# Hybrid decoder step: sample states of the gated-delta layer as the moving operand, 32-column strips stationary, results used in place

## The chip, the cores and the metric

The kernel runs on one NeuronCore of a Trainium2 chip. The metric is the device time of one execution in microseconds (us); lower is better. Before the change the median of three runs is 2275.27 us (2274.68 to 2281.68).

## What is computed

One inference step of a four-layer decoder trunk (retention, Mamba-2 SSD, gated DeltaNet, retention), each layer followed by a squared-ReLU MLP. 256 prompt tokens and 8 sample sequences of 4 tokens each go through the same weights, so that every dense product has 288 token columns. Only the gated-delta layer (the third) is touched, and in it only the sample part. For one sample sequence and one of the 16 heads, with the state S (128 x 128) from the input, the reference does this over its single chunk of four tokens:

```python
v_new = u_c - jnp.einsum('bhtk,bhkv->bhtv', w_c, S)
o_c = jnp.einsum('bthk,bhkv->bthv', qd_c, S) + jnp.einsum('bhts,bhsv->bthv', attn_c, v_new)
S = S * cd_c[..., None, None] + jnp.einsum('bshk,bhsv->bhkv', kd_c, v_new)
```

`u_c` and `w_c` are the solutions of a unit lower triangular 4 x 4 system per head and sequence (right sides: values and decayed keys, both times beta). `o_c` is then normalised over its 128 elements. Two heads that follow each other share q and k.

## The kernel before

Everything is fp32. The large dense products (`dense`, lines 190 to 227) take their weights through `raw` tiles from HBM, split each into a rounded part `wh` (ACT, L207) and a rest `wl` (DVE, L210), and do three matmuls per 128 x 128 weight tile with 288 moving columns (L222, L223, L224, output `psd`). These fill most of the program; the scans of the mixers are put between them.

The gated-delta layer works in four units of four heads (`units`). A unit m has `proj(m)` (dense products and convolution for q, k, v), `prep(m)` (grams, the triangular inverses, gates), `loop(m)` (the prompt scan in two chunks), `sample(m)` (the sample sequences), `gate(m)` and `fin(m)`, and the output product `out`. `weave` runs prep and loop as a chain; each of their yields is a wait that is filled with dense blocks, `proj(m+1)` and `sample(m)` (both in turn), in the fourth unit with `sample(3)` alone after `gate(3)` and `out(1)`. The yields of `sample` count as filled time. A scheduler then sets the final order of each engine's instructions, so that the order on an engine is not that of the code; two PSUM banks carry the tag `s`, which `sample` and the small matmuls of `prep` use in turn.

`sample(m)` (lines 1570 to 1612) goes over two pairs of heads. For each head it loads the eight states as `St` (128 x 8 x 128, L1584) and does eight matmuls with a state as the stationary operand and eight columns of `qk` (k and q, four tokens each) as the moving one:

```python
for b in range(DB):
    mm(pv[:, h, b], St[:, b], qk[:, pr:4:2, SEQ + b:T:DB])
yield 1.8
```

The result `ps_kS` is (value index x columns). ACT copies it into `kS` in two pieces (L1590), two matmuls with the identity transpose it (`ps_u2`), DVE forms the right side `r2` with a scale and the values `vb2` (L1595), ACT scales the q part to `qo` (L1597), one matmul with the inverse `Y2` gives v_new (`ps_n2`, copied to `x4`, L1601), one with `at2` gives the inner part (`ps_o2`), and DVE adds `qo` to make `o2` (L1605). Square and sum (L1608), the mean (DVE, L1610), a power on POOL (L263) and a scaled copy to `on2` (L1612) finish it; `fin` transposes `on2` (L1730) for the gate. All matmuls of this layer's scan go through the helper `mm` at L1296. In the trace buffer names lose trailing digits: `ps_u2` is ps_u, `ps_n2` ps_n, `ps_o2` ps_o (with input lkv, which is `x4`), `Y2` Y, `at2` at, `o2` o, `on2` on.

`prep` makes `sc2`, `vb2`, `Y2` (the inverse, transposed) and `at2`; `er` is a small tile of decays (L1387) that POOL multiplies with q into `qd`.

Of the kernel before, what the change touches and what calls it, by code (L numbers as in the profile page):

```python
# [8 lines left out]
F32 = mybir.dt.float32  # L9
F32R = mybir.dt.float32r  # L10
I32 = mybir.dt.int32
AF = mybir.ActivationFunctionType
ALU = mybir.AluOpType
# [3 lines left out]
SEQ = 256  # L17
DB, DS = 8, 4
NS = DB * DS
T = SEQ + NS  # L20
# [15 lines left out]
def make_consts():  # L36

    f = np.float32
    c = {}
# [3 lines left out]
    u = np.arange(NS)  # L43
# [5 lines left out]
    t = np.arange(SEQ)  # L49
# [39 lines left out]
    x = np.arange(128)  # L89
# [18 lines left out]
    c["gdn_lms"] = np.stack(lms, axis=1).astype(f)  # L108
    same = jx[:, None] == ub[None, :]
    c["gdn_m4"] = np.stack([same & (jt[:, None] <= ut[None, :]), same & (ut[None, :] < jt[:, None])], axis=1).astype(f)  # L110
    u1 = np.zeros((128, 2, 128), f)
    for h in range(4):
        for blk in range(4):
# [10 lines left out]
class K:  # L124
# [1119 lines left out]
    def gdn(self, ctx, j, i):  # L1244
# [5 lines left out]
        V, A, G, PE = nc.vector, nc.scalar, nc.gpsimd, nc.tensor  # L1250
        ident = self.ident

        def cload(name):
            a = I[name]
            t = cp.tile(list(a.shape), F32, name="c_" + name)
            nc.sync.dma_start(t, a)
            return t

        b32, lms, gmask, m4, xi0, h16 = (cload(n) for n in ("gdn_b32", "gdn_lms", "gdn_gm", "gdn_m4", "gdn_x0", "gdn_h16"))
        i4, s4 = m4[:, 0], m4[:, 1]  # L1260
        istk = cp.tile([128, 16], F32, name="istk")
        nc.sync.dma_start(istk, I["ssd_istk"][:, 0:16])
# [29 lines left out]
        def bcm(ap, n):  # L1292
            return ap.unsqueeze(1).broadcast_to([ap.shape[0], n, ap.shape[1]])

        def mm(o, l, r, start=True, stop=True):
            PE.matmul(o, lhsT=l, rhs=r, start=start, stop=stop)  # L1296
# [57 lines left out]
        T64 = rp.tile([64, 8, 64], F32, name="T64")  # L1354
        G.memset(T64, 0.0)

        def proj(m):
            qk = rp.tile([128, 4, T], F32, name="qk", tag="qk", bufs=2)
            v = [rp.tile([128, T], F32, name="v", tag=f"v{a}") for a in range(4)]
            tails, tl = [], rp.tile([128, 8, 35], F32, name="tl", tag="tl", bufs=2)  # L1360
            for (c0, dst) in ((m * 256, [qk[:, 0], qk[:, 1]]), (1024 + m * 256, [qk[:, 2], qk[:, 3]]), (2048 + m * 512, v)):
                yield from self.conv_dense(rp, xh, xl, w[:, c0:c0 + len(dst) * 128], c0 // 128, rb, cw, cb, None, dst, tails, tl)
            units[m] = {"qk": qk, "v": v, "tails": tails}
# [7 lines left out]
        def prep(m):  # L1371
# [4 lines left out]
            for kh in range(2):  # L1376
                ps = self.ps("ps_dif", "s")
                h0 = 4 * m + 2 * kh
                for r in range(2):
                    mm(ps[:, r * 256:(r + 1) * 256], e2[:, h0 + r:h0 + r + 1].broadcast_to([128, 128]), cts)  # L1380
                Et = rp.tile([128, 2, 2, 128], F32, name="Et", tag=f"Et{kh}")
                pv = ps.rearrange("p (r t y) -> p r t y", r=2, t=2)
                for r in range(2):
                    for tt in range(2):
                        A.activation(Et[:, r, tt], pv[:, r, tt], AF.Abs, bias=nct[:, tt, h0 + r:h0 + r + 1])
                er = rp.tile([128, 2, 128], F32, name="er", tag="er")
                A.activation(er, pv[:, :, 1], AF.Exp)  # L1387
                e_ = Et.rearrange("p r t y -> p (r t y)")
                A.activation(e_, e_, AF.Exp, scale=-1.0)
                G.tensor_tensor(out=qd[:, 2 * kh:2 * kh + 2], in0=er, in1=bcm(qk[:, kh, 128:256], 2), op=ALU.mult)  # L1390
                Es.append(Et)
            rb2 = rp.tile([128, 32], F32, name="rb2", tag="rb2")
            V.tensor_scalar(out=rb2, in0=i4, scalar1=g2[:, m:m + 1], scalar2=None, op0=ALU.mult)
            ps = self.ps("ps_dif2", "s")
# [154 lines left out]
            def expand(k, t):  # L1549
# [16 lines left out]
            at2 = rp.tile([128, 128], F32, name="at2", tag="at2")  # L1566
            G.tensor_tensor(out=at2.rearrange("p (c y) -> p c y", c=4), in0=bcm(sm[:, 0], 4),
                            in1=b32.rearrange("p (c y) -> p c y", c=4), op=ALU.mult)
            u.update(Tm=Tm, L=L, at=Es, qd=qd, kd=kd, vb=vbs, ncf=ncf, eq=eq, sc2=sc2, Y2=Y2, x4=x4, vb2=vb2, at2=at2)

        def sample(m):
            u = units[m]
            while "x4" not in u:
                yield None
            qk, Y2, x4, vb2, at2, sc2, eq = (u[n] for n in ("qk", "Y2", "x4", "vb2", "at2", "sc2", "eq"))
            on2 = u["on2"] = rp.tile([128, 128], F32, name="on2", tag="on2")
            for pr in range(2):
                hp = slice(64 * pr, 64 * pr + 64)

                pT = self.ps("ps_kS", "s")  # L1580
                pv = pT[:, 0:128].rearrange("p (h b c) -> p h b c", h=2, b=DB)
                for h in range(2):
                    St = rp.tile([128, DB, 128], F32, name="St", tag="St", bufs=3)
                    nc.sync.dma_start(St, I["state_gdn"][j, :, 4 * m + 2 * pr + h].rearrange("b k v -> k b v"))  # L1584
                    for b in range(DB):
                        mm(pv[:, h, b], St[:, b], qk[:, pr:4:2, SEQ + b:T:DB])
                    yield 1.8
                kS = rp.tile([128, 2, 64], F32, name="kS", tag="kS", bufs=2)
                for a in range(2):
                    A.copy(kS[:, a].rearrange("p (h t b) -> p h b t", h=2, b=DB), pv[:, :, :, 4 * a:4 * a + 4])  # L1590
                pu = self.ps("ps_u2", "s")
                for a in range(2):
                    mm(pu[hp, a * 128:(a + 1) * 128], kS[:, a], ident)
                qo, r2, o2 = (rp.tile([128, 128], F32, name=n_, tag=n_) for n_ in ("qo", "r2", "o2"))
                V.scalar_tensor_tensor(out=r2[hp], in0=pu[hp, 128:256], scalar=sc2[hp, 2:3], in1=vb2[hp], op0=ALU.mult,  # L1595
                                       op1=ALU.add)
                A.activation(qo[hp], pu[hp, 0:128], AF.Copy, scale=eg2[hp, m:m + 1])  # L1597
                yield 1.0
                pn = self.ps("ps_n2", "s")
                mm(pn[hp, 0:128], Y2[hp, hp], r2[hp])  # L1600
                A.copy(x4[hp, 1], pn[hp, 0:128])  # L1601
                yield 1.0
                po = self.ps("ps_o2", "s")
                mm(po[hp, 0:128], at2[hp, hp], x4[hp, 1])
                V.tensor_tensor(out=o2[hp], in0=qo[hp], in1=po[hp, 0:128], op=ALU.add)  # L1605
                yield 1.0
                oo = rp.tile([128, 1], F32, name="oo1", tag="oo1", bufs=2)
                A.activation(qo[hp], o2[hp], AF.Square, accum_out=oo[hp])  # L1608
                ms = rp.tile([128, 1], F32, name="ms1", tag="ms1", bufs=2)
                V.scalar_tensor_tensor(out=ms[hp], in0=oo[hp], scalar=1.0 / 128, in1=eq[hp, 4:5], op0=ALU.mult, op1=ALU.add)  # L1610
                r = self.rsqrt(ms, hp)
                A.activation(on2[hp], o2[hp], AF.Copy, scale=r[hp])  # L1612

        def loop(m):
            u = units[m]
# [212 lines left out]
```

## Time and profile before

| | |
|---|---|
| median of three runs | 2275.27 us |
| the profiled execution | 2272.98 us, of which the span from first to last instruction is 2271.1 us |
| mean granted TensorE clock | 0.978 |
| gated-delta layer | about 1096 to 1497 us of the span |

The engines are PE (matmul) with PEld (its weight loads), DVE (VectorE), ACT (ScalarE), POOL (GpSimd) and SP (which issues most transfers). A row of the timeline gives the start, the length from the first start to the last end, and how many instructions were merged; lengths of neighbours overlap, because matmuls are pipelined, so that the pace is read from start to start. A group of matmuls carries its array shape (rows\*columns used by the stationary operand) and the moving operand. An fp32 matmul of the scan stands in the trace as two records; those of `psd` as one.

### The profile page before, as it was taken

To read this page: it belongs to the slowest core of one execution; us is meant where nothing else is said; L and a number is where in the kernel's file an instruction comes from. 1 tells how busy PE (TensorE), PEld (TensorE's weight loads), DVE (VectorE), ACT (ScalarE), POOL (GpSimd) and SP (SyncE) were. 2 spreads that over 40 slices of the span, in tenths; PEclk is the share of its full clock that TensorE was granted. 3 is DMA by queue.
4 is the path that set the end of the run, shared out by engine and by line. 5 is a ranking of instruction groups with operands and counts; after the bars stand their busy time and mean duration, and the time that the engine had idled before them with its cause. 6 is when DMAs were issued, how large, how long until landed. Compare 5 with 4: busy or idle time off the path is not lost. (4 is left out here: it accounts for less than half of the span.)

```text
span 2271.1 us, 43130 instructions
## 1 busy us (share of the span) xinstructions
PE 2186.3 (96%) x16332; PEld 2019.0 (89%) x16332; DVE 1562.4 (69%) x3211; ACT 1243.3 (55%) x2827; POOL 580.0 (26%) x605
## 2 busy tenths in 40 slices
PE   9999999998999999999898999989999999999998
PEld 7878899997889889999788987889999878889998
DVE  6777775557888877555886686466766677776554
ACT  4444455554767765545566566366644345445454
POOL 2100113332332222333322122034433001103333
PEclk9999999999999999999899999799999999999999
DMA  7876755545446545545443432257765666664553
GB/s 207 266 255 205 246 186 165 167 153 157 139 146 178 170 128 167 167 150 167 126 133 100 131 120 81 84 156 241 234 204 183 226 231 215 239 232 149 167 167 114
DMA packets 404076, 394.83 MB, mean 174 GB/s; under 512 B 12988, under 2 KB 353573, under 8 KB 403773
## 3 DMA queue, kind: packets, MB, share of 16 engines
q1 hardware_dynamic: 403708, 391.82, 54.3%
q8 instruction: 128, 2.10, 0.4%
q14 instruction: 80, 0.65, 0.1%
q10 hardware_dynamic: 96, 0.20, 0.0%
q0 software_dynamic: 64, 0.07, 0.0%
HBM read 333.36 MB, written 58.69 MB: 173 GB/s over the span
## 5 line engine op out<-in xcount | busy, mean ns | idle before, releaser
L207 ACT CAST wh<-raw 128x512 fp32r<-128x512 f32 x1024 | 627.8, 621 | 687.5 <-PE psd L223 642.5
L210 DVE TENSOR_TENSOR wl<-raw,wh 128x512 fp32r<-128x512 f32 x1024 | 744.3, 734 | 316.3 <-ACT wh L207 292.9
L222 PE MATMUL psd<-xh,wh 128*128 128x288 f32 x2576 | 775.4, 302 | 6.4 <-ACT xh L297 4.6
L224 PE MATMUL psd<-xh,wl 128*128 128x288 f32 x2576 | 771.6, 300 | 4.7 <-DVE wl L210 4.3
L223 PE MATMUL psd<-xl,wh 128*128 128x288 f32 x2576 | 771.0, 300 | 4.0 <-DVE xl L298 3.2
L222 PEld LDWEIGHTS psd<-xh,wh 128*128 128x128 f32 x2576 | 487.1, 189 | 25.1 <-issue 9.6
L223 PEld LDWEIGHTS psd<-xl,wh 128*128 128x128 f32 x2576 | 490.6, 190 | 17.6 <-issue 8.1
L224 PEld LDWEIGHTS psd<-xh,wl 128*128 128x128 f32 x2576 | 489.4, 190 | 13.4 <-DVE wl L210 7.6
L222 PE MATMUL psd<-ah,wh 128*128 128x288 f32 x1536 | 463.5, 302 | 10.0 <-DVE sg L543 3.7
L224 PE MATMUL psd<-ah,wl 128*128 128x288 f32 x1536 | 460.5, 300 | 4.1 <-DVE wl L210 4.0
L223 PE MATMUL psd<-al,wh 128*128 128x288 f32 x1536 | 461.6, 301 | 0.4 <-DVE al L465 0.4
L222 PEld LDWEIGHTS psd<-ah,wh 128*128 128x128 f32 x1536 | 293.9, 192 | 18.9 <-DVE x L442 4.2
L223 PEld LDWEIGHTS psd<-al,wh 128*128 128x128 f32 x1536 | 294.0, 191 | 9.6 <-issue 7.4
L224 PEld LDWEIGHTS psd<-ah,wl 128*128 128x128 f32 x1536 | 294.6, 192 | 7.6 <-DVE wl L210 5.5
L482 POOL TENSOR_TENSOR x<-x,dn 128x288 f32<-128x288 f32 x120 | 149.2, 1243 | 233.2 <-DVE dn L480 233.2
L463 POOL TENSOR_TENSOR a<-v 128x288 f32<-128x288 f32 x128 | 110.2, 861 | 271.9 <-ACT v L462 267.6
L726 DVE SCALAR_TENSOR_TENSOR S<-S,ps_up 128x512 f32<-128x512 f32 x128 | 83.5, 685 | 53.4 <-PE ps_up L725 50.7
L827 DVE SCALAR_TENSOR_TENSOR cacc<-U,cw,cacc 128x312 f32<-128x312 f32 x192 | 106.4, 561 | 8.2 <-ACT cacc L822 5.9
L465 DVE TENSOR_TENSOR al<-a,ah 128x288 fp32r<-128x288 f32 x128 | 59.0, 461 | 67.2 <-POOL a L463 66.5
L263 POOL TENSOR_TENSOR rs_y<-ms,mhalf 128x3 f32<-128x3 f32 (+3 forms) x37 | 36.7, 995 | 237.6 <-DVE ms L742 170.6
L803 POOL COPY U<-cb 128x24 f32<-128x24 f32 x64 | 34.1, 538 | 218.0 <-DVE cacc L827 120.5
L480 DVE TENSOR_TENSOR dn<-psd,rb 128x288 f32<-128x288 f32 x128 | 58.2, 455 | 40.0 <-PE psd L224 40.0
(504 smaller groups left out, 2651.7 us busy)
## 6 DMA issues: line engine op xcount, KB each, us to landing
raw<-mlp_w_up SPq DMA_DIRECT2D x64, 1024.0 KB
raw<-mlp_w_down SPq DMA_DIRECT2D x64, 1024.0 KB
raw<-ret_w_in SPq DMA_DIRECT2D x32, 1024.0 KB
S<-state_ret SPq DMA_DIRECT2D x64, 512.0 KB
s_ret<-S SPq DMA_DIRECT2D x64, 512.0 KB
raw<-ssd_w_in SPq DMA_DIRECT2D x24, 1024.0 KB
raw<-gdn_w_in SPq DMA_DIRECT2D x24, 1024.0 KB
raw<-ret_w_in SPq DMA_DIRECT2D x32, 512.0 KB
```

The source lines that it names most:

```text
L207: self.last_cast = nc.scalar.copy(wh, src)
L210: nc.vector.tensor_tensor(out=wl, in0=src, in1=wh, op=ALU.subtract)
L222: nc.tensor.matmul(po, lhsT=hs[k][:, os], rhs=xh[k], start=(k == 0), stop=False)
L223: nc.tensor.matmul(po, lhsT=hs[k][:, os], rhs=xl[k], start=False, stop=False)
L224: self.last_mm = nc.tensor.matmul(po, lhsT=ls[k][:, os], rhs=xh[k], start=False, stop=(k == kt - 1))
L263: self.nc.gpsimd.tensor_tensor(out=y[rows], in0=ms[rows], in1=self.mhalf[rows].broadcast_to([rows.stop - rows.start, n]), op=ALU.pow)
L463: nc.gpsimd.tensor_tensor(out=a, in0=v, in1=v, op=ALU.mult)
L465: nc.vector.tensor_tensor(out=al[o], in0=a, in1=ah[o], op=ALU.subtract)
L480: nc.vector.tensor_tensor(out=t, in0=ps, in1=rb2, op=ALU.mult)
L482: e.tensor_tensor(out=self.x[o], in0=self.x[o], in1=t, op=ALU.add)
L726: nc.vector.scalar_tensor_tensor(out=S[:, b, z], in0=S[:, b, z], scalar=C["g4"][h], in1=up, op0=ALU.mult, op1=ALU.add)
L827: nc.vector.scalar_tensor_tensor(out=acc[:, 0:n], in0=u, scalar=wk, in1=acc[:, 0:n], op0=ALU.mult, op1=ALU.add)
```

## The change

- In `sample` the state `St[:, b]` becomes the moving operand (128 columns). Stationary is a strip of 32 columns from a new tile `Z`, in which the k and q columns of sequence b stand at their places and all else is zero. Sequence b writes the partitions 32\*(b % 4) and up of `ps_kS`; b and b + 4, and the two heads, accumulate into the same strip. The result is (rows x value index), already the right way round.
- `ps_u2`, `r2`, `qo` (as a scaled q part) and `o2` go. The rows of `kS` are used in place: `prep` makes `WQ`, two 128 x 128 matrices that hold the scaled inverse and the scaled identity with their rows scattered by a constant `pm` (two matmuls `ps_wq`, two ACT scalings and an ACT copy per unit). `ps_n2` and `ps_o2` become two accumulating matmuls each: `WQ` by `kS` and the earlier one.
- The square and the final scaling read `ps_o2` in PSUM, which so stays taken until `on2` is written.
- POOL fills `Z` (four copies per unit and a memset at the layer's start); `er` is written into `qd` and multiplied there in place.
- The yield after a head's matmuls goes from 1.8 to 1.0; the one behind `kS` stays at 1.0. One constant of 128 KB more is loaded.

```diff
+        Z = rp.tile([128, 2, DB, 40], F32, name="Z")
+        G.memset(Z, 0.0)
...
-                er = rp.tile([128, 2, 128], F32, name="er", tag="er")
+                er = qd[:, 2 * kh:2 * kh + 2]
...
+            for pr in range(2):
+                for bh in range(2):
+                    bs = slice(4 * bh, 4 * bh + 4)
+                    G.tensor_copy(Z[:, pr, bs, 8:40].rearrange("p b (a x) -> p b a x", a=2)[:, :, :, bs],
+                                  qk[:, pr:4:2, SEQ:T].rearrange("p a (t b) -> p b a t", b=DB)[:, bs])
...
+            t0, t1 = self.t128("wy"), self.t128("wq")
+            A.activation(t0, Y2, AF.Copy, scale=sc2[:, 2:3])
+            A.activation(t1, ident, AF.Copy, scale=eg2[:, m:m + 1])
+            WQ = rp.tile([128, 2, 128], F32, name="WQ", tag="WQ")
+            ps = self.ps("ps_wq", "s")
+            for a, t in enumerate((t0, t1)):
+                mm(ps[:, 128 * a:128 * a + 128], pm[:, a], t)
+            A.copy(WQ.rearrange("p a x -> p (a x)"), ps[:, 0:256])
...
                     for b in range(DB):
-                        mm(pv[:, h, b], St[:, b], qk[:, pr:4:2, SEQ + b:T:DB])
-                    yield 1.8
-                kS = rp.tile([128, 2, 64], F32, name="kS", tag="kS", bufs=2)
-                for a in range(2):
-                    A.copy(kS[:, a].rearrange("p (h t b) -> p h b t", h=2, b=DB), pv[:, :, :, 4 * a:4 * a + 4])
-                pu = self.ps("ps_u2", "s")
-                for a in range(2):
-                    mm(pu[hp, a * 128:(a + 1) * 128], kS[:, a], ident)
-                qo, r2, o2 = (rp.tile([128, 128], F32, name=n_, tag=n_) for n_ in ("qo", "r2", "o2"))
-                V.scalar_tensor_tensor(out=r2[hp], in0=pu[hp, 128:256], scalar=sc2[hp, 2:3], in1=vb2[hp], op0=ALU.mult,
-                                       op1=ALU.add)
-                A.activation(qo[hp], pu[hp, 0:128], AF.Copy, scale=eg2[hp, m:m + 1])
+                        c = 32 * (b % 4)
+                        mm(pT[c:c + 32, 0:128], Z[:, pr, b, 8 - 8 * h:40 - 8 * h], St[:, b], h == 0 and b < 4, h == 1 and b > 3)
+                    yield 1.0
+                kS = rp.tile([128, 128], F32, name="kS", tag="kS", bufs=2)
+                A.copy(kS, pT[:, 0:128])
                 yield 1.0
                 pn = self.ps("ps_n2", "s")
-                mm(pn[hp, 0:128], Y2[hp, hp], r2[hp])
+                mm(pn[hp, 0:128], WQ[:, 0, hp], kS, True, False)
+                mm(pn[hp, 0:128], Y2[hp, hp], vb2[hp], False, True)
                 A.copy(x4[hp, 1], pn[hp, 0:128])
                 yield 1.0
                 po = self.ps("ps_o2", "s")
-                mm(po[hp, 0:128], at2[hp, hp], x4[hp, 1])
-                V.tensor_tensor(out=o2[hp], in0=qo[hp], in1=po[hp, 0:128], op=ALU.add)
+                mm(po[hp, 0:128], WQ[:, 1, hp], kS, True, False)
+                mm(po[hp, 0:128], at2[hp, hp], x4[hp, 1], False, True)
```

Two places of the order on PE. The names are those of the trace; psd are the dense products, ps_kS the matmuls with the states, ps_u the transposes with the identity, ps_n and ps_o as above, ps_W (first two forms) and ps_v small matmuls of `prep`.

The first place is in the fourth unit: the second pair of heads before the change.

```order
L1296 MATMUL ps_o_18703<-lkv,at_18439 64x128
L1296 MATMUL ps_kS<-qk,St 128x8 x16
L224 MATMUL psd<-ah_17880,wl 128x288
L222 MATMUL psd<-ah_17881,wh 128x288
L223 MATMUL psd<-al_17885,wh 128x288
L1296 MATMUL ps_u_18737<-c_ident,kS 64x128
L224 MATMUL psd<-ah_17881,wl 128x288
L222 MATMUL psd<-ah_17882,wh 128x288
L223 MATMUL psd<-al_17886,wh 128x288
L1296 MATMUL ps_u_18737<-c_ident,kS 64x128
```

And the same unit, from the end of the first pair's chain to the second pair's states, with the change:

```order
L1302 MATMUL ps_n_18697<-kS,WQ 64x128
L1302 MATMUL ps_n_18697<-vb_18378,Y_18405 64x128
L1302 MATMUL ps_o_18701<-kS,WQ 64x128
L227 MATMUL psd<-ah_17875,wh 128x288
L228 MATMUL psd<-al_17879,wh 128x288
L1302 MATMUL ps_o_18701<-lkv,at_18436 64x128
L1302 MATMUL ps_kS<-St,Z 32x128 x8
L229 MATMUL psd<-ah_17875,wl 128x288
L1302 MATMUL ps_W_18216<-Ls,L 32x16 x32
L1548 MATMUL ps_v<-c_ident,v 128x128 x4
L1302 MATMUL ps_W_18216<-Ls,Tm 32x16 x32
L1548 MATMUL ps_v<-c_ident,v 128x128 x4
```

The transposes are gone, the two heads of the pair no longer stand in one run of 16, and the small matmuls of `prep` come between them.

The second place is the end of the fourth unit, `fin(3)`: before the change

```order
L1728 MATMUL ps_oT<-c_ident,on 128x128 x2
L1729 MATMUL ps_oT<-c_ident,on 128x128 x2
L1728 MATMUL ps_oT<-c_ident,on 128x128
L1729 MATMUL ps_oT<-c_ident,on 128x128
L1730 MATMUL ps_oT<-c_ident,on_18631 128x32 x3
L1728 MATMUL ps_oT<-c_ident,on 128x128
L1729 MATMUL ps_oT<-c_ident,on 128x128
L1730 MATMUL ps_oT<-c_ident,on_18631 128x32
```

and with it, from the row that follows 16 dense rows behind the first `ps_oT`:

```order
L1748 MATMUL ps_oT<-c_ident,on 128x128
L227 MATMUL psd<-ah_17876,wh 128x288
L1748 MATMUL ps_oT<-c_ident,on 128x128
L228 MATMUL psd<-al_17880,wh 128x288
L229 MATMUL psd<-ah_17876,wl 128x288
L227 MATMUL psd<-ah_17877,wh 128x288
L1747 MATMUL ps_oT<-c_ident,on 128x128
L1748 MATMUL ps_oT<-c_ident,on 128x128
L228 MATMUL psd<-al_17881,wh 128x288
```

Before, no dense row stood among the transposes; now 16 stand behind the first two of them and 11 more among the rest.

## Rows read from the trace of the kernel before

**Rows 1.** The page: engine, busy us (share of the span), instructions.
```profile
PE 2186.3 (96%) x16332; PEld 2019.0 (89%) x16332; DVE 1562.4 (69%) x3211; ACT 1243.3 (55%) x2827; POOL 580.0 (26%) x605
```

**Rows 2.** A stretch: its us, PE, PEld, DVE, ACT, POOL busy; clock, DMA share, GB/s.
```profile
1180.00:1216.00 36.00, 35.07 (x443) 31.45 (x441) 22.40 (x57) 24.07 (x70) 6.29 (x11) 1.00 0.33 100
```

**Rows 3.** Who PE waited for, 1096 to 1482 us: total us, times, longest.
```profile
PE ps_Y L1554 <- DVE T L1553: 4.2, 2, 3.0
```

**Rows 4.** Timeline of PE around the first head's states: start us, length us.
```profile
1168.36 0.29 PE L224 MATMUL psd<-xh,wl 128*128 128x288 f32 x1
1168.49 1.84 PE L1296 MATMUL ps_kS<-qk,St 128*128 128x8 f32 x16
1170.19 0.38 PE L222 MATMUL psd<-xh,wh 128*128 128x288 f32 x1
1170.40 0.29 PE L223 MATMUL psd<-xl,wh 128*128 128x288 f32 x1
```

**Rows 5.** Timeline of PE around eight matmuls with 32 stationary, 128 moving columns.
```profile
1140.89 0.29 PE L224 MATMUL psd<-xh,wl 128*128 128x288 f32 x1
1141.11 0.65 PE L1296 MATMUL ps_qs<-c_ident,qk 128*32 128x128 f32 x16
1141.69 0.40 PE L222 MATMUL psd<-xh,wh 128*128 128x288 f32 x1
1141.92 0.29 PE L223 MATMUL psd<-xl,wh 128*128 128x288 f32 x1
```

**Rows 6.** Timeline of PE around strips whose moving operands differ (retention).
```profile
77.00 1.05 PE L717 MATMUL ps_yi<-S,qm 128*32 128x512 f32 x4
77.98 0.40 PE L223 MATMUL psd<-xl,wh 128*128 128x288 f32 x1
```

**Rows 7.** Timeline of PE around the two transposes ps_u.
```profile
1178.32 0.29 PE L224 MATMUL psd<-xh,wl 128*128 128x288 f32 x1
1178.54 0.65 PE L1296 MATMUL ps_u<-c_ident,kS 128*64 128x128 f32 x4
1179.12 0.40 PE L222 MATMUL psd<-xh,wh 128*128 128x288 f32 x1
```

**Rows 8.** Timeline of PE around one matmul ps_n.
```profile
1356.40 0.43 PE L1296 MATMUL ps_n<-r,Y 64*64 64x128 f32 x2
1356.76 0.40 PE L222 MATMUL psd<-xh,wh 128*128 128x288 f32 x1
```

**Rows 9.** Timeline of PE around four full matmuls with 128 moving columns.
```profile
1469.32 1.05 PE L1296 MATMUL ps_vn<-vb,Ye 128*128 128x128 f32 x8
1470.13 0.38 PE L224 MATMUL psd<-ah,wl 128*128 128x288 f32 x1
```

**Rows 10.** Groups of instructions, ACT: a 128x128 scaling; busy us, mean ns, idle before.
```profile
L1542 ACT ACTIVATE vb<-ps_v,sc 128x128 f32<-128x128 f32 x4 | 1.5, 363 | 1.2 <-PE ps_v L1296 1.2
```

**Rows 11.** The page's groups, POOL: a small copy (columns as in Rows 10).
```profile
L803 POOL COPY U<-cb 128x24 f32<-128x24 f32 x64 | 34.1, 538 | 218.0 <-DVE cacc L827 120.5
```

**Rows 12.** Stretches of the fourth unit (columns as in Rows 2).
```profile
1425.90:1432.80 6.90, 6.90 (x32) 6.90 (x33) 2.13 (x8) 0.65 (x3) 0.00 (x0) 0.51 0.31 81
1432.80:1443.00 10.20, 10.20 (x75) 9.20 (x75) 7.27 (x28) 3.72 (x7) 0.00 (x0) 1.00 0.55 189
1443.00:1456.70 13.70, 13.70 (x54) 11.27 (x54) 4.31 (x12) 2.38 (x8) 0.00 (x0) 0.50 0.03 12
```

**Rows 13.** Timeline of PE, states of the fourth unit's second pair.
```profile
1441.20 5.38 PE L1296 MATMUL ps_kS<-qk,St 128*128 128x8 f32 x32
```

**Rows 14.** Who PE waited for, 1479 to 1500 us.
```profile
PE ps_oT L1729 <- ACT on L1684: 2.9, 1, 2.9
PE ps_oT L1730 <- ACT on L1612: 1.6, 1, 1.6
```

**Rows 15.** Timeline, all engines: the end of one pair's chain.
```profile
1217.41 0.43 PE L1296 MATMUL ps_o<-lkv,at 64*64 64x128 f32 x2
...
1220.28 0.40 ACT L1612 ACTIVATE on<-o,rs_y 64x128 f32<-64x128 f32 x1 [0.77 <-POOL rs_y L263]
```

More of the change, by code (lines that the diff above doesn't have):

```diff
@@ L110, in make_consts @@
     c["gdn_m4"] = np.stack([same & (jt[:, None] <= ut[None, :]), same & (ut[None, :] < jt[:, None])], axis=1).astype(f)
+    pm = np.zeros((128, 2, 128), f)
+    for a in range(2):
+        pm[x, a, 32 * (x % 4) + 16 * (1 - a) + 8 * (x // 32 % 2) + 4 * (x % 8 // 4) + x % 32 // 8] = 1.0
+    c["gdn_pm"] = pm
     u1 = np.zeros((128, 2, 128), f)
@@ L1257, in cload @@
             return t
-        b32, lms, gmask, m4, xi0, h16 = (cload(n) for n in ("gdn_b32", "gdn_lms", "gdn_gm", "gdn_m4", "gdn_x0", "gdn_h16"))
+        b32, lms, gmask, m4, xi0, h16, pm = (cload(n) for n in ("gdn_b32", "gdn_lms", "gdn_gm", "gdn_m4", "gdn_x0",
+                                                                "gdn_h16", "gdn_pm"))
         i4, s4 = m4[:, 0], m4[:, 1]
@@ L1389, in prep @@
                 A.activation(e_, e_, AF.Exp, scale=-1.0)
-                G.tensor_tensor(out=qd[:, 2 * kh:2 * kh + 2], in0=er, in1=bcm(qk[:, kh, 128:256], 2), op=ALU.mult)
+                G.tensor_tensor(out=er, in0=er, in1=bcm(qk[:, kh, 128:256], 2), op=ALU.mult)
                 Es.append(Et)
+            for pr in range(2):
[3 more added lines that the diff above has]
+                                  qk[:, pr:4:2, SEQ:T].rearrange("p a (t b) -> p b a t", b=DB)[:, bs])
             rb2 = rp.tile([128, 32], F32, name="rb2", tag="rb2")
@@ L1568, in prep @@
                             in1=b32.rearrange("p (c y) -> p c y", c=4), op=ALU.mult)
-            u.update(Tm=Tm, L=L, at=Es, qd=qd, kd=kd, vb=vbs, ncf=ncf, eq=eq, sc2=sc2, Y2=Y2, x4=x4, vb2=vb2, at2=at2)
+            t0, t1 = self.t128("wy"), self.t128("wq")
[6 more added lines that the diff above has]
+            A.copy(WQ.rearrange("p a x -> p (a x)"), ps[:, 0:256])
+            u.update(WQ=WQ, Tm=Tm, L=L, at=Es, qd=qd, kd=kd, vb=vbs, ncf=ncf, eq=eq, sc2=sc2, Y2=Y2, x4=x4, vb2=vb2, at2=at2)
         def sample(m):
@@ L1574, in sample @@
                 yield None
-            qk, Y2, x4, vb2, at2, sc2, eq = (u[n] for n in ("qk", "Y2", "x4", "vb2", "at2", "sc2", "eq"))
+            Y2, x4, vb2, at2, WQ, eq = (u[n] for n in ("Y2", "x4", "vb2", "at2", "WQ", "eq"))
             on2 = u["on2"] = rp.tile([128, 128], F32, name="on2", tag="on2")
@@ L1580, in sample @@
                 pT = self.ps("ps_kS", "s")
-                pv = pT[:, 0:128].rearrange("p (h b c) -> p h b c", h=2, b=DB)
                 for h in range(2):
@@ L1603, in sample @@
                 po = self.ps("ps_o2", "s")
-                mm(po[hp, 0:128], at2[hp, hp], x4[hp, 1])
-                V.tensor_tensor(out=o2[hp], in0=qo[hp], in1=po[hp, 0:128], op=ALU.add)
+                mm(po[hp, 0:128], WQ[:, 1, hp], kS, True, False)
+                mm(po[hp, 0:128], at2[hp, hp], x4[hp, 1], False, True)
                 yield 1.0
                 oo = rp.tile([128, 1], F32, name="oo1", tag="oo1", bufs=2)
-                A.activation(qo[hp], o2[hp], AF.Square, accum_out=oo[hp])
+                qo = self.t128("qo")
+                A.activation(qo[hp], po[hp, 0:128], AF.Square, accum_out=oo[hp])
                 ms = rp.tile([128, 1], F32, name="ms1", tag="ms1", bufs=2)
@@ L1611, in sample @@
                 r = self.rsqrt(ms, hp)
-                A.activation(on2[hp], o2[hp], AF.Copy, scale=r[hp])
+                A.activation(on2[hp], po[hp, 0:128], AF.Copy, scale=r[hp])
         def loop(m):
```

## The prediction

> **What bounds the kernel now.** I read the page's busy times first, then the stretches of the gated-delta layer, then who PE waited for, then the timeline of PE around each matmul that the change touches. PE is busy 96% of the span, DVE 69%, ACT 55% [rows 1]. That alone says little, since matmul lengths overlap. The stretches say more: where the sample heads stand between the steps of the prompt scan, PE is busy 35.07 of 36 us, DVE 22.4, ACT 24.1, and the DMA queues a third of the time [rows 2]. There PE is the bound, and what it saves is saved. Elsewhere in the layer PE waits for DVE (3.0 us in one place for the inverse's first step [rows 3]); a saving just before such a wait is given back.
>
> The pace of the dense rows is 0.13 us from start to start [rows 4], so I price an insertion as the time from the dense row before it to the second dense row behind it, less 0.27 us for the two dense rows in there. This takes in what PE loses on entry and exit.
>
> **The change, part by part.**
>
> *States.* One head costs 1170.40 - 1168.36 - 0.27 = 1.77 us; the 16 records follow each other at 1.70/16 = 0.106 us although only eight columns move, so loading the state is what is paid [rows 4]. With the change a head is eight matmuls with 32 stationary and 128 moving fp32 columns, over four strips. The trace has exactly this form in ps_qs: 1141.92 - 1140.89 - 0.27 = 0.76 us [rows 5]. There the moving operand is the identity each time; here it is another state each time. In the retention layer strips with different states as moving operand, accumulating, stand as well: four matmuls of 512 columns in 0.98 us [rows 6]. With full arrays four fp32 matmuls of 128 columns take 0.81 us [rows 9], so that 512 columns one after the other would take over 3 us; the strips do run side by side. I take 0.76. There are 16 heads: 16 x 1.01 = **-16.2 us**. Lower bound of the gain: none, if the strips did not overlap (below).
>
> *Transposes.* ps_u costs 0.58 us, plus entry (0.22 against 0.13) and exit as in the strips (0.23 against 0.13) [rows 5], 0.77 in all [rows 7]; 8 of them: **-6.2 us**.
>
> *Two matmuls more per pair.* ps_n and ps_o each get an accumulating partner with 128 moving columns. Two such matmuls in a row take 0.58 [rows 7], one 0.36 [rows 8]; the second is worth 0.22. In the order 13 of the 16 partners stand side by side; three are split by dense rows or a transpose and pay their own entry and exit, 0.36 + 0.09 + 0.10 = 0.55. 13 x 0.22 + 3 x 0.55 = **+4.5 us**; bounds 3.5 (all 0.22) and 8.8 (all 0.55).
>
> *WQ.* Four full matmuls of 128 columns take 0.81 us [rows 9], so ps_wq about 0.4 plus 0.1 of entry and exit, four times: **+2.0 us**. It waits for two ACT scalings of 0.36 us behind the inverse [rows 10]; in the order 9 to 21 dense rows (1.2 to 2.8 us) stand between, which hide them. Without that cover: 0.7 us each time, 3 us in all. Only the first ps_n of a unit reads WQ, later still.
>
> *ACT, DVE, POOL, SP.* Two copies become one, the scaled q goes, three operations per unit come: about nothing on ACT, which has a third of its time free where this stands [rows 2]. DVE loses two small operations per pair, not on its late side; nothing. POOL gets 16 copies, by the nearest row 0.54 us each [rows 11], 9 us on an engine busy a quarter of the time; the four of a unit stand ahead of the power that the next norm waits for, and some wait for the last states of the unit before. The POOL work behind them is not needed until the grams; I take 0, bound +2 us (one copy in each unit exposed). `er` in place makes ACT wait where POOL did; the readers of the old `qd` end before `fin` transposes their results, so 0. The constant's load (128 KB) hides among the megabyte loads of the MLP before: 0.
>
> *The clock.* In the fourth unit the pairs' heads stand together, 32 records of eight moving columns in 5.4 us [rows 13], and the granted clock is 0.50, the lower of the two levels (1.2 GHz of 2.4), for 6.9 us from within the first such run and for 13.7 us from within the second [rows 12]. Between them 75 records take 10.2 us, 0.136 each; at that pace the 32 and 54 records of the slow stretches would take 4.4 and 7.3 us, so the slow clock costs 2.5 + 6.4 = 8.9 us. The new order has no such run: the second pair's heads are apart, and strips keep four times the columns moving. But ps_W with 32x16 forms stands there instead. I take half, **-4.5 us**; bounds 0 and -8.9. The Trainium skill (TensorE: Matmul & The Clock Gate, Part 1) says that the throttled state is the default and activity releases it; the half clock inside a run in which PE never idles shows that being busy is not enough for that here.
>
> *The layer's end.* PE waits 2.9 and 1.6 us for ACT at the last transposes [rows 14], the second time for `on` of the second pair, whose sum stood late on DVE. That sum is gone and the two scalings now stand together ahead of it; and 27 dense rows (3.6 us) stand among the transposes, 16 of them right under the first wait. **-3 us**; bounds 0 and -4.5.
>
> *What becomes visible.* With shorter insertions the hops from states to copy to ps_n to copy to ps_o have less beside them; in the fourth unit there are two or three dense rows (0.3 to 0.4 us) per hop, against an ACT step with its hand-overs. Eight pairs with about 0.5 us each: **+4 us**; bounds 0 and +8.
>
> Sum: -16.2 - 6.2 + 4.5 + 2.0 - 4.5 - 3 + 4 = -19.4 us, from 2273.0 to 2253.6 us on the profiled execution. That execution is 2.3 us under the median of the three runs (2275.3) and under each of them; on the median this is about 2256 us.
>
> **The rivals.**
>
> *Swallowed by waits.* PE's saving runs into waits for DVE and ACT that stay where they are, the clock falls as before and the end is as long. For it: the layer's preparation stretches with their waits [rows 3]. Against it: the heads stand where PE has 1 us free in 36 [rows 2]. Half of the PE sum (-15.9) is left: 2275.3 - 8 = 2267 us.
>
> *Everything comes.* The clock stays up (-8.9), the end closes (-4.5), nothing becomes visible: -15.9 - 8.9 - 4.5 = -29.3, 2246 us.
>
> *The strips run one after another.* Then a head's 16 records take 0.10 us each [rows 9], 1.6 us and the states gain nothing: -6.2 + 4.5 + 2.0 - 3 + 2 = about -1, 2274 us: no change. Rows 5 and 6 speak against it. The Trainium skill (FP8 and Floating Point Precision, TensorE Precision Notes) gives true fp32 four passes through the array; counted so, 128 moving columns cost as much as the state's load did, and the change would be worth nothing on the states unless strips overlap, which the trace shows they do.
>
> *The PSUM bank held (slower).* `ps_o2` is now read until `on2` is written. From the matmul to the start of that scaling the shortest case takes 1220.28 - 1217.41 + 0.40 = 3.3 us [rows 15]. Two banks carry the tag, so the next matmul but one that asks for it, ps_n of the second pair or the second decay matmul of the next `prep`, must wait for `on2`. Priced in full, eight times 3.3 = 26 us, against the gain of 19.4: 2282 us. It decides from 3.3 us per pair on (19.4 + 6.8 over eight). Against it: in the order the states, the other chunk's matmuls or 10 dense rows stand in between, and one DVE step of the chain is gone.
>
> **How the numbers follow.** A difference under 0.3% (6.8 us) can't be told from none here. Forecast 0.57; everything comes 0.14; swallowed 0.20; strips serial 0.05; bank held 0.04. Faster takes the first two and 0.16 of the swallowed case (it centres 1.5 us beyond the bound): 0.87. Same: 0.04 of it and the serial case, 0.09. Slower 0.04. The range must leave out no more than 0.2: 2245 to 2269 takes in the forecast with its bounds on the clock (-4.4), the end and the hops (+4), the swallowed case, and the low case; the last two rivals stay out.
>
> **What would show it.** ps_kS with St as moving operand: 256 records of 128\*32, 128x128, about 0.58 us per head in the timeline; no ps_u with kS; ps_n and ps_o of four records, 0.6 us; ps_wq without idle before it. Clock near 1.00 from 1425 us to the layer's end; transposes ps_oT with less than 2 us of idle. It would be wrong if a head took over 1 us, if PE's waits in the layer grew by over 10 us, or if rows of ps_n or the decays were released by `on`.

## The result, and the profile after

On the first chip the change takes 2246.17 us (median of four executions, 2242.83 to 2250.74) and the kernel before 2278.47 us (four, 2274.68 to 2282.71): ratio 0.9859, 95% interval 0.983 to 0.9888. That is 32 us less; the forecast was about 20 less and 2256 us. The profiled execution of the change took 2250.74 us, its span is 2248.6 us; it is the slowest of its four, while the one profiled before, 2272.98 us, lies below the four of the kernel before here. Between the two traces the gain is 22 us.

The page of the change, engines (answers to [rows 1]):

```profile
PE 2172.1 (97%) x16348; PEld 1996.7 (89%) x16348; DVE 1555.2 (69%) x3195; ACT 1242.9 (55%) x2823; POOL 586.0 (26%) x622
```

PE is still the bound. One head's states, timeline of PE (start, length, instruction; answers to [rows 4]):

```profile
1176.39 0.29 PE L229 MATMUL psd<-xh,wl 128*128 128x288 f32 x1
1176.61 0.65 PE L1302 MATMUL ps_kS<-St,Z 128*32 128x128 f32 x16
1177.19 0.40 PE L227 MATMUL psd<-xh,wh 128*128 128x288 f32 x1
1177.42 0.29 PE L228 MATMUL psd<-xl,wh 128*128 128x288 f32 x1
```

From the dense row before to the second behind, less two dense rows: 1177.42 - 1176.39 - 0.27 = 0.76 us, as taken from ps_qs [rows 5], against 1.77 before. The strips run side by side with different states too. Further on in the same trace stand the two pairs of accumulating matmuls (answers to [rows 8]):

```profile
1214.59 0.29 PE L229 MATMUL psd<-xh,wl 128*128 128x288 f32 x1
1214.81 0.43 PE L1302 MATMUL ps_n<-kS,WQ 128*64 128x128 f32 x2
1215.18 0.43 PE L1302 MATMUL ps_n<-vb,Y 64*64 64x128 f32 x2
1215.54 0.43 PE L1302 MATMUL ps_o<-kS,WQ 128*64 128x128 f32 x2
1215.90 0.40 PE L227 MATMUL psd<-xh,wh 128*128 128x288 f32 x1
```

Here each matmul takes 0.36 to 0.37 us from start to start; the second one is not cheaper, as I had it. The array shapes differ (128 rows, then 64), and e2 below bears this out.

Who PE waited for in the scan (from the layer's first gram to the first update of a state, 1150 to 1494 us; total, times, longest; the same stretch before held [rows 3] and [rows 14]):

```profile
PE psd L229 <- DVE wl L215: 6.8, 4, 2.6
PE ps_Y L1569 <- DVE T L1568: 4.1, 3, 2.9
PE ps_oT L1748 <- ACT on L1703: 2.5, 3, 1.1
PE ps_S L1302 <- ACT vn L1677: 1.4, 3, 0.6
...
PE ps_oT L1749 <- ACT on L1631: 0.9, 2, 0.5
PE ps_n L1302 <- ACT kS L1614: 0.2, 1, 0.2
```

The hops of the pairs that I feared show up with 0.2 us in all (`ps_n` for `kS`; `ps_o` waits nowhere, and `ps_wq` neither). The same view of the kernel before, over its own scan, shows what has gone:

```profile
PE psd L224 <- DVE wl L210: 4.4, 3, 2.1
...
PE psd L222 <- DVE sg L543: 3.7, 1, 3.7
PE ps_oT L1729 <- ACT on L1684: 3.7, 2, 2.9
PE ps_oT L1730 <- ACT on L1612: 3.4, 4, 1.6
PE ps_S L1296 <- ACT vn L1658: 3.0, 4, 1.5
```

The two waits of the transposes `ps_oT` for `on` fall from 7.1 to 3.4 us over the four units, the one for `sg` (3.7) is gone, that for `vn` halves; the wait for `wl` grows by 2.4. At the layer's end alone, 1450 to 1497 us, where [rows 14] had 2.9 and 1.6 us, the change has:

```profile
PE ps_oT L1748 <- ACT on L1703: 1.0, 1, 1.0
```

Stretches of the change (length; busy us of PE, PEld, DVE, ACT, POOL; granted clock; DMA share; GB/s), among them two that answer to [rows 2] and [rows 12]:

```profile
1190.00:1226.00 36.00, 34.76 (x333) 30.42 (x327) 20.40 (x48) 24.84 (x74) 7.54 (x12) 1.00 0.30 97
1425.00:1430.90 5.90, 4.79 (x136) 3.67 (x129) 1.25 (x3) 4.30 (x14) 0.78 (x2) 1.00 0.29 110
1430.90:1448.00 17.10, 17.10 (x110) 14.30 (x110) 2.89 (x6) 5.31 (x13) 0.00 (x0) 0.50 0.01 1
1448.00:1494.00 46.00, 43.87 (x318) 41.32 (x318) 30.90 (x61) 34.00 (x85) 16.85 (x16) 1.00 0.53 154
```

Against the forecast the clock does fall to 0.50 (1.2 of 2.4 GHz) once in the fourth unit, for 17.1 us; from 1448 us on it stays up to the scan's end. Before the change there was one more such stretch that the forecast left out of its sum, right behind the wait of 2.9 us at the last transposes:

```profile
1484.00:1494.20 10.20, 8.51 (x36) 7.82 (x36) 4.50 (x11) 3.82 (x11) 0.55 (x1) 0.50 0.23 67
```

With the change that wait and that stretch are both gone.

The same sums for the traces that matter, PE from start to start over the scan, a gap of over 0.6 us counted as a wait less 0.13. "Low" is the time at the lower clock level in the scan; e6 is the kernel before again and e1 the change again (below):

| us | before | e6 (before) | change | e1 (change) |
|---|---|---|---|---|
| execution | 2273.0 | 2284.8 | 2250.7 | 2247.5 |
| scan | 370.9 | 378.6 | 344.2 | 342.6 |
| states | 30.2 | 31.9 | 10.9 | 10.9 |
| `ps_u` | 6.1 | 6.0 | 0 | 0 |
| `ps_n`, `ps_o` | 6.2 | 6.2 | 12.6 | 12.6 |
| `ps_wq` | 0 | 0 | 2.1 | 2.1 |
| dense rows | 217.1 | 221.9 | 215.0 | 213.8 |
| other matmuls | 82.7 | 85.6 | 83.3 | 83.3 |
| waits | 28.6 | 26.9 | 20.4 | 19.8 |
| low | 44 | 65 | 31 | 27 |

Of the dense rows there are as many in each column: what their sum changes by is mostly the clock, with the entry and exit of the matmuls put among them and waits under 0.6 us in it as well. Between the profiles before and after, the scan loses 26.7 us, 4 more than the execution; the rest of the program is that much longer, and the scan starts 2.3 us later (1150.1 against 1147.8 us), but in e6, the kernel before again, it starts later still (1152.1). Between e6 and e1 the scan loses 36.0 us: the touched matmuls 18.5, dense rows 8.1, other matmuls 2.3, waits 7.1.

### The profile page after: what moved, and what is told of

Read it like the earlier page. It is cut to its first block, busy times and chain, and to the rows that moved or that the text cites. A ratio compares the mean times of both kernels' runs of the same rounds, so it can differ in the third digit from the quotient of the medians.

```text
span 2248.6 us, 43174 instructions
## 1 busy us (share of the span) xinstructions
PE 2172.1 (97%) x16348; PEld 1996.7 (89%) x16348; DVE 1555.2 (69%) x3195; ACT 1242.9 (55%) x2823; POOL 586.0 (26%) x622
## 5 line engine op out<-in xcount | busy, mean ns | idle before, releaser
L229 PEld LDWEIGHTS psd<-ah,wl 128*128 128x128 f32 x1536 | 293.9, 191 | 10.2 <-DVE wl L215 9.1
```

The lines of the kernel that those rows point to most:

```text
L229: self.last_mm = nc.tensor.matmul(po, lhsT=ls[k][:, os], rhs=xh[k], start=False, stop=(k == kt - 1))
```

## The experiments

All ratios are to the kernel before, run on the same chip. e1 to e4 ran on one chip (before: 2283.25 us), e5 to e8 on one (2280.96), e9 to e11 on one (2280.53), e12 by itself (2281.17). Of the kernels made from the change, only e2 has the change's order; in e3, e4, e7 and e12 the scheduler's order differs on PE, DVE, ACT and POOL, so that their times hold the edit and another order together.

**e1, the change once more**, unedited.

> The change once more, to narrow its interval. Theory (PE is the bound, the sum of the PE pieces of the layer is the gain): the trace of the layer is 26.7 us shorter than before (states -19.3, transposes -6.1, partners +6.3, WQ +2.1, waits over 0.6 us -8.2, dense rows -2.1), so 24 to 29 us under the kernel before, ratio 0.987 to 0.990. Rival (something outside the layer's PE pieces gains too, or the executions so far were lucky): ratio at or under 0.985, with a gain in the trace outside 1147 to 1500 us.

2241.64 us (2240.06 to 2247.46), ratio 0.9819 (0.9806 to 0.9832), some 42 us less. The two intervals just touch; the gain lies between 32 and 42 us, above the forecast in both. The theory's 24 to 29 us is missed: the pieces of the first two traces are not the whole gain (e5 and e6).

**e2, the second matmuls with 128 rows.** The columns of `Y2` and `at2` outside their block are zero for these rows, so that the result is the same, and the order on every engine stays.

```diff
-                mm(pn[hp, 0:128], Y2[hp, hp], vb2[hp], False, True)
+                mm(pn[hp, 0:128], Y2[:, hp], vb2, False, True)
...
-                mm(po[hp, 0:128], at2[hp, hp], x4[hp, 1], False, True)
+                mm(po[hp, 0:128], at2[:, hp], x4[:, 1], False, True)
```

> The partners' second matmul (Y2 by vb2, at2 by x4) takes all 128 rows, as WQ does; the other pair's rows meet zeros, so the result is the same, and the order on every engine is the change's. Theory (the partners cost 0.72 us per group of four records, against 0.58 for two matmuls of one shape, because PE changes its array shape between them): ps_n groups fall from 0.72 to 0.58 us, 13 side-by-side groups of 16 gain 0.14 us and a little on entry, 2 us in all; ratio to the change about 0.999. Rival (the second matmul waits for its operand instead): 0.72 stays, no gain.

Timeline of PE in e2:

```profile
1215.96 0.43 PE L1302 MATMUL ps_n<-kS,WQ 128*64 128x128 f32 x2
1216.23 0.38 PE L1302 MATMUL ps_n<-vb,Y 128*64 128x128 f32 x2
1216.45 0.38 PE L1302 MATMUL ps_o<-kS,WQ 128*64 128x128 f32 x2
```

0.27 and 0.22 us instead of 0.37 and 0.36: with one array shape the second matmul does cost 0.22. A pair ahead of a dense row takes 0.58 us (1185.06 to 1185.64) where the change has 0.72 (1183.76 to 1184.48), so two shapes cost about 0.14 a pair. The edit also raises the rows from 64 to 128, so it does not separate the shape from the rows; that 16 records of 64\*64 with 64 columns follow each other in 1.07 us in the change (`ps_W`, 1193.88 to 1194.95) speaks against the rows alone. `ps_n` and `ps_o` fall from 12.6 to 9.3 us over the scan. The time does not follow: 2243.8 us, ratio 0.9835 (0.9821 to 0.985), an interval that overlaps that of e1. Three us of PE are below what the executions of one kernel differ by.

**e3, the strips alone.** States as the moving operand, but then as before: two matmuls gather the rows of `kS` (with `pm` transposed, as the transposes did), `r2`, `qo` and `o2` as before; no `WQ`, no accumulating partners.

```diff
-                    mm(pu[hp, a * 128:(a + 1) * 128], kS[:, a], ident)
+                    mm(pu[hp, a * 128:(a + 1) * 128], pm[:, 1 - a, hp], kS)
```

> The strips alone: states as the moving operand, but the rows of kS are gathered by two matmuls per pair with a constant (in place of the transposes with the identity), and r2, the scaled q and o2 are made as before the change; no WQ, no partners. Theory (PE sum): against the change PE saves the partners (6.3) and WQ (2.1) and pays the gathers (0.77 x 8 = 6.2): 2 us faster to equal if the longer chain stays hidden; so 24 to 28 us under the kernel before. Rival (the shorter chain in place is worth something, as the waits over 0.6 us fell by 8.2 us): the waits come back and it is 4 to 8 us slower than the change.

2242.07 us, ratio 0.982 (0.9806 to 0.9833): that of the change itself. The transposes saved are paid for by the partners and `WQ` (-6.1 against +6.4 and +2.1 in the table); the results used in place bring nothing that can be measured, the strips, with the order that comes with them, bring all.

**e4, one strip.** All eight sequences add into the same 32 rows, the other rows of `kS` are set to zero, so that the results of the sequences are mixed.

```diff
-                        c = 32 * (b % 4)
+                        c = 0
```

> All eight sequences of a head write the same 32 partitions instead of four strips, so that their matmuls cannot stand side by side; the copy to kS takes those 32 rows, the rest of kS is zeros (POOL memset). It sums the sequences into one another, so sample outputs are not the reference's. Theory (the gain of the states rests on strips that overlap): a head takes 16 x 0.10 = 1.6 us or more instead of 0.57, 16 x 1.05 = 17 us slower than the change, 9 us under the kernel before at most. Rival (32 stationary columns load quicker, overlap does not matter): a head stays under 0.9 us, within 5 us of the change.

One head in e4, timeline of PE:

```profile
1175.92 0.29 PE L229 MATMUL psd<-xh,wl 128*128 128x288 f32 x1
1176.14 1.94 PE L1302 MATMUL ps_kS<-St,Z 128*32 128x128 f32 x16
1178.01 0.40 PE L227 MATMUL psd<-xh,wh 128*128 128x288 f32 x1
```

1.87 us from start to start where the change has 0.58: four strips at once are worth a factor of 3.2. The Trainium skill (TensorEngine Tiling (Array Packing), Stationary-Streaming Swap + Column Tiling) names this swap, with four-fold column tiling for 32 columns; the trace agrees, with 3.2 in place of four. The time is 2260.36 us, ratio 0.9909 (0.9891 to 0.9927), 18.7 us over e1. So the overlap is worth what the table gives the states. But in e4 the states cost PE as much as before (30.8 us of the scan), and it still is 23 us faster than the kernel before, not 9 at most as expected. More than half of the gain is not the shorter states.

**e5 and e6, the kernel before again**, each with one profile, unedited.

> The kernel before, profiled once more. Its profiled execution (2273.0 us) was 5 to 16 us under its timed ones, so part of the measured gain (41 us beside the kernel before in the last comparison, 27 in the traces) is not in that trace. Theory (the clock): an execution nearer the median spends some 20 us more at the lower level of the clock in the gated-delta layer than the 58 us of the first trace, near the runs of ps_kS, and 5 us or more of extra time stand in its dense rows there. Rival (the rest of the program varies): the layer takes the 371 us it took, and the extra time stands outside it.

> The same kernel, a third profile, with the same two expectations: a layer of over 376 us with more low clock in it (theory), or a layer of 371 us and the difference elsewhere (rival).

2283.77 and 2284.82 us, with the same scan to 0.1 us (378.6). Stretches of e5:

```profile
1366.00:1372.40 6.40, 6.34 (x169) 5.69 (x167) 4.57 (x12) 5.27 (x16) 1.79 (x3) 1.00 0.55 168
1372.40:1392.90 20.50, 20.50 (x150) 17.80 (x149) 5.55 (x14) 7.96 (x23) 0.00 (x0) 0.50 0.24 71
```

and what PE did where it begins:

```profile
1370.47 1.84 PE L1296 MATMUL ps_kS<-qk,St 128*128 128x8 f32 x16
1372.17 0.38 PE L222 MATMUL psd<-xh,wh 128*128 128x288 f32 x1
1372.38 0.39 PE L223 MATMUL psd<-xl,wh 128*128 128x288 f32 x1
1372.70 1.06 PE L1296 MATMUL ps_W<-Ye,L 32*32 32x32 f32 x30
```

Right after a head with eight moving columns, amid small matmuls of `prep`, the clock goes to the lower level for 20.5 us. The trace on which I forecast has 3.4 us there. It is an execution that was spared. The same holds beyond the profiles: over all executions of e1 to e12's comparisons the mean granted clock is 0.970 to 0.980 for the kernel before, the slower ones lower, and 0.980 to 0.984 for the change (first chip and e1); the profile of before had 0.978.

**e7, every head's matmuls twice**, so that the products with the states count double.

```diff
+                    for z in range(2):
                         for b in range(DB):
```

> The change with each head's eight matmuls done twice into the same sums, so that sample results are not the reference's. 16 records more per head, at 0.44 us per 16 behind one another (0.57 less the lead-out). Theory (PE is the bound, what PE spends is spent): 16 x 0.44 = 7 us slower than the change. Rival (waits for DVE and ACT take up small PE differences, as they took the 2 us of the full-row partners): within 3 us of the change.

2262.14 us, ratio 0.9919 (0.9892 to 0.9945): 16 to 20 us more than the two medians of the change, for 7.6 us more of states and 7 expected. The rest: 41 us low instead of 27 to 31, waits of 23.4 instead of 20, other matmuls 86.9 instead of 83.3. Something beside the states' own length decides; the order differs too, and why the clock falls at other places there stays open.

**e8 and e11, 64 moving columns.** The kernel before with each state's matmul eight times as wide: the eight columns, and seven copies that later matmuls overwrite or nobody reads. The result is the same, and the load of the state, which sets the pace, too.

```diff
-                        mm(pv[:, h, b], St[:, b], qk[:, pr:4:2, SEQ + b:T:DB])
+                        o = 64 * h + 8 * b
+                        mm(pT[:, o:o + 64].rearrange("p (r a t) -> p r a t", r=8, a=2), St[:, b],
+                           qk[:, pr:4:2, SEQ + b:T:DB].unsqueeze(1).broadcast_to([128, 8, 2, 4]))
```

> The kernel before with 64 moving columns per state in place of 8: the eight true columns come first, seven copies follow, which the next matmul overwrites, so that the result is the reference's. The load of the state still sets the pace (64 columns at 0.1 us per 128). Theory (eight moving columns let the clock fall): less low clock in the layer, and 5 to 12 us faster than before in spite of more work. Rival (the clock does not depend on the columns moved): the same time as before within 4 us, with as much low clock. The scheduler's order shifts a little, since it counts the wider matmuls otherwise.

> e8 once more, on the same chip as e9 and e10: ratio about 0.99 by both theories; its time at the lower level (27 us in e8) is what e9 and e10 are held against.

2253.66 us, ratio 0.9894 (0.9862 to 0.9925), and 2253.21 us, ratio 0.9885 (0.9862 to 0.9908). Eight times the columns make the kernel before 27 us faster, more than the 5 to 12 expected. But the scheduler, which goes by estimated lengths, had also put the instructions in another order; hence the next two.

**e9 and e10, columns and order apart.** At the end of the program order-only edges are added between each engine's instructions, which hold them in the order of the other kernel: e9 is the kernel before (eight columns) in the order of e8, e10 is e8 (64 columns) in the order of before. Apart from the moving operand, e9 and e11 have the same instructions in the same order on every engine, and so have e10 and the kernel before.

```diff
         K(ctx, tc, I, O, C, layers).run()
+        in_order(tc)
```

> The kernel before, eight moving columns per state, but every engine's instructions held in the order that the kernel with 64 moving columns had (e8). Theory that the narrow matmuls pull the granted clock down, whatever the order: TensorE is at the lower level for 60 to 80 us of the gated-delta layer and the time is that of the kernel before (ratio 0.995 to 1.005). Rival, the order made the gain of e8: the time is that of e8, ratio about 0.99, with about 27 us at the lower level. If both share it, a ratio between and 40 to 55 us.

> 64 moving columns per state (seven copies are overwritten, the result is the same), every engine's instructions in the order of the kernel before. Theory that the columns decide: about 27 us at the lower level, ratio about 0.99 (27 us faster than before). Rival, the order: 60 to 80 us at the lower level and the time of the kernel before, or some us more.

| median us | order of before | order of e8 |
|---|---|---|
| 8 columns | 2280.53 | 2267.12 (e9, ratio 0.9949, 0.9929 to 0.9969) |
| 64 columns | 2267.71 (e10, ratio 0.9942, 0.9921 to 0.9963) | 2253.21 (e11) |

Neither theory alone: each step is worth 13 to 14 us, and on the medians they add up. The ten executions of e9 fall into two groups, 2261.0 to 2262.1 and 2266.7 to 2273.0 us, with a mean clock of 0.978 to 0.980 and 0.973 to 0.976; its profile below is the slowest of them, so that the long fall it shows stands for the slower group. (The expectations count the lower level from 1090 to 1500 us: 58 us in the first trace of before, and 68, 38 and 21 us in e9, e10 and e11. From here on it is the scan alone.) The scan as one stretch, first e9, then e10, then e11:

```profile
1150.50:1516.80 366.30, 347.84 (x3180) 318.00 (x3180) 252.53 (x659) 221.54 (x595) 86.93 (x114) 0.93 0.35 110
```

```profile
1151.70:1510.40 358.70, 333.20 (x3180) 305.05 (x3179) 251.62 (x659) 220.81 (x594) 87.36 (x114) 0.98 0.37 116
```

```profile
1150.50:1498.60 348.10, 331.08 (x3181) 302.72 (x3180) 252.46 (x659) 221.78 (x595) 87.47 (x114) 0.99 0.37 116
```

What the columns do is seen in e9 and e11 at one place. In e9 the run of 32 states of the fourth unit, and the stretches around it:

```profile
1430.44 4.74 PE L1296 MATMUL ps_kS<-qk,St 128*128 128x8 f32 x32
1435.03 0.59 PE L222 MATMUL psd<-ah,wh 128*128 128x288 f32 x1
```

```profile
1425.00:1432.70 7.70, 7.70 (x64) 7.70 (x63) 6.86 (x26) 2.48 (x4) 0.00 (x0) 1.00 0.40 139
1432.70:1466.80 34.10, 34.10 (x328) 29.28 (x328) 6.62 (x18) 10.45 (x31) 0.78 (x2) 0.50 0.14 48
```

And the same run in e11, with 64 columns:

```profile
1426.71 3.79 PE L1296 MATMUL ps_kS<-qk,St 128*128 128x64 f32 x32
1430.25 0.38 PE L222 MATMUL psd<-ah,wh 128*128 128x288 f32 x1
```

```profile
1425.00:1432.70 7.70, 7.70 (x62) 7.00 (x60) 6.13 (x22) 1.99 (x5) 0.00 (x0) 1.00 0.43 140
1432.70:1466.80 34.10, 31.83 (x421) 28.48 (x420) 12.59 (x31) 18.12 (x49) 4.93 (x7) 1.00 0.18 61
```

With eight columns the clock falls inside the run and stays at the lower level for 34.1 us; with 64 it stays up, the run takes 3.54 us instead of 4.59, and 421 instructions pass in the 34.1 us instead of 328. PE was busy, by the profile, without a gap for the 7.7 us before the fall. The Trainium skill (TensorE: Matmul & The Clock Gate, HAM oscillation) puts such a fall down to gaps in which PE is idle; there is none here, so that account does not cover this fall. Against the kernel before, e10 (same order) has 17 us low for 44 to 65, and dense rows of 210.8 us for 217.1 to 221.9, while its waits stay at 27.3 us. That is the clock alone. Not all low time belongs to the narrow matmuls: e10 keeps the wait of 2.9 us at the last transposes, and with it a stretch at the lower level.

```profile
1477.90:1484.70 6.80, 5.26 (x23) 5.26 (x24) 3.52 (x9) 2.28 (x7) 0.55 (x1) 0.50 0.07 20
```

What the order does is seen in the waits, 8 to 9 us of its 13 to 14: 19.4 us in e9 and 17.9 in e11, against 27 to 28.6 for before and 27.3 for e10. Of e10:

```profile
PE ps_oT L1732 <- ACT on L1614: 3.7, 4, 1.9
PE psd L222 <- DVE sg L543: 3.7, 1, 3.7
PE ps_oT L1731 <- ACT on L1686: 3.7, 2, 2.9
PE ps_S L1296 <- ACT vn L1660: 3.0, 4, 1.5
```

and of e9:

```profile
PE psd L222 <- DVE sg L543: 2.2, 1, 2.2
PE ps_S L1296 <- ACT vn L1658: 1.5, 3, 0.6
PE ps_oT L1730 <- ACT on L1612: 1.4, 2, 0.7
PE ps_oT L1729 <- ACT on L1684: 1.0, 1, 1.0
```

It is the same four waits that shrank with the change, here with the old sample part untouched.

**e12, the PSUM bank given back early.** DVE copies `ps_o2` to `on2`; the square and the last scaling read that.

```diff
+                V.tensor_copy(on2[hp], po[hp, 0:128])
-                A.activation(qo[hp], po[hp, 0:128], AF.Square, accum_out=oo[hp])
+                A.activation(qo[hp], on2[hp], AF.Square, accum_out=oo[hp])
```

> The change, but DVE copies ps_o2 to on2 at once, and the square and the last scaling read on2, so that the PSUM bank comes free after one copy instead of after the scaling. Theory that the held bank costs nothing: the ratio to the kernel before stays that of the change (0.980 to 0.985). Rival, the bank held: the matmuls of the next pair or of the next prep start earlier, and the ratio falls to 0.978 or lower (some 10 us of the 26 us that the full price would be). A slower result, 0.986 or more, would be the extra DVE step in the chain at the layer's end.

2250.16 us (2241.63 to 2253.86), ratio 0.9867 (0.9836 to 0.9897). Not faster: the held bank costs nothing that this copy would give back. Its executions are spread over 12 us, and its order differs from the change's, so whether the extra DVE step costs a little stays open, though 0.9867 lies where the expectation put that cost. The change's own waits speak for a free bank as well: PE waits for `on` at `ps_oT` alone, not at `ps_n` or at the decays.

No version beats the change by more than its uncertainty; e2 and e3 equal it.

## Why the prediction was right or wrong

The 2246.17 us lie inside the range of 2245 to 2269 us by 1 us only; the repetition e1, 2241.64 us, lies under it. So the forecast gave too little, and two of its steps say why.

*Faster, and by which matmuls: right.* The insertion of a head is 0.76 us, as forecast, and over the scan the states lose 19.3 us (forecast 16.2 at full clock; some two of the other three are states that had run at the lower level, since e11, nearly all at full clock, has 28.2 us; the table also counts a head from start to start, 1.70 and 0.58 us, where the forecast took entry and exit in, 1.77 and 0.76). Transposes -6.1 (forecast -6.2), `ps_wq` +2.1 (+2.0).

*The partners: mis-sized.* +6.4 instead of +4.5 us, within the bounds. I priced the second matmul at 0.22 from two of one shape; with two shapes it costs 0.36 (e2).

*The end of the layer: right.* The wait at the last transposes falls from 4.5 us [rows 14] to 1.0, 3.5 us less; forecast 3.

*"What becomes visible", +4 us: this step failed.* It put a wait at each hop; there is 0.2 us in all. In place of it the new order took 4 to 5 us more of waits away than the end accounts for (8.2 in all), above all the 3.7 us for `sg`. The order of e8 does much the same without the change (e9); how much of the change's gain its own order makes is not shown, since no run holds it to the old one. I read the change's new order only at the places of the sample part, and gave no term to what it does for waits elsewhere.

*The clock, -4.5 us: right in sign, mis-sized for most executions.* Between the two profiles 14 us fewer are low, 10.2 of them the stretch behind the wait at the layer's end, which had no term. Between e6 and e1 it is 38 us fewer, with 8.1 us less of dense rows alone. Where I had a doubt for the change, since `ps_W` stands there in place of the states, the clock did fall, for 17.1 us at 1431 us. That `ps_W` is the cause is not shown: PE had been busy for 4.79 of the 5.9 us ahead of it only, and e2, in the change's order, has the full clock at that place:

```profile
1425.00:1450.00 25.00, 23.10 (x368) 19.47 (x369) 8.82 (x22) 13.90 (x37) 2.85 (x4) 1.00 0.21 66
```

*The step from the profile to the median: this failed, too, and makes most of the miss.* On the profiled execution the forecast was 2253.6 us, and the profile of the change took 2250.7. I took the 2.3 us by which the profiled execution lay under its median as a constant; the change's profile lies 4.6 us over its median, the slowest of four. Of the 10 us between 2256 and 2246.17 that is 7, and 3 are the forecast on the profile. As for the gain, the execution profiled before had little time at the lower clock; e5 and e6 lose 7.7 us more in the scan. What most executions lose there the change mostly removes (65 us low in e6, 27 to 31 with the change); that the narrow matmuls were the main cause is shown by e10 for the kernel before and argued from it for the change. So the gain of the medians (32 to 42 us) is larger than that of the two traces (22).

*The rivals.* Swallowed by waits: no, the waits became less. Everything comes (2246 us): the median, but by luck, since the clock did fall once and the waits gave more than its sum had. Strips one after another: they overlap; and the 2274 us set on that case were wrong: e4 takes 2260, since there too the clock stays up (14 us low) and the waits are 20.2 us. Bank held: e12 and e3, which gives it back as before, show no cost.

## What to carry to other kernels

Where matmuls with few moving columns come in runs, look at the granted clock of the dense work behind them: the loss stands there, not in the narrow instructions, and wider moving operands, or the swap of moving and stationary, can bring back time of the same order as the shorter instructions do: 13 us here (e10 against the kernel before), beside 19 (e1 against e4). Before a forecast, profile the old kernel more than once if its executions differ by more than the term at stake. And keep the work and the order apart in an experiment, since a scheduler that goes by lengths can answer a change of size with another order, as it did in e8.

## What was not expected of the hardware

- Seven useless copies made a kernel 27 us faster (e8, e11): 13 us by the clock in an unchanged order (e10), the rest by the order that came with them.
- A PE busy for 7.70 of 7.70 us, the last 2.3 of them with eight-column matmuls, dropped to 1.2 GHz for 34.1 us; with 64 columns at the same place it did not.
- Two array shapes in place of one cost about 0.14 us a pair of matmuls (0.72 us for `ps_n` and its partner, 0.58 with one shape, e2).
